# First token tile's logits in two products instead of three, both tiles' meta probabilities in one transpose, and the last square of the feed-forward norm added on POOL

## The chip, the cores and the metric

The kernel runs on one core of a Trainium2 chip. The metric is the device time of one execution in microseconds (us); the median of the runs shown counts.

## What is computed

One decoder block on 256 tokens of width 1024, in float32. 16 learned meta tokens stand ahead, so 272 positions (L) go through the block. What matters here, cut from the reference:

```python
proj = rmsnorm(h, norm_mix_g) @ w_in          # q, k, v, indexer, convolution, gates
# 8 heads of width 128; each query sees the keys that the indexer's top-k selects
logits = einsum('bthd,btkhd->bthk', q_b, k_sel) * HEAD_DIM ** -0.5
p = softmax(where(valid, logits, -inf))
y_attn = einsum('bthk,btkhd->bthd', p, v_sel).reshape(b, l, ATTN_WIDTH) @ w_attn_out
mixed = sigmoid(ga) * y_attn + sigmoid(gb) * y_conv
h = h + mixed @ w_out
f = rmsnorm(h, norm_ffn_g)
h = h + (silu(f @ w_gate) * (f @ w_up)) @ w_down
out = rmsnorm(h, norm_final_g)[:, N_META:]
```

## The kernel before

Weights come in 159 *units*, blocks of 128 rows by 1024 columns, in the order of `UNITS`. For each unit SyncE loads the block (`raw`), ACT copies it to a rounded high part (`whi`, L162), DVE subtracts to get the low part (`wlo`, L170), four units ahead of their use, and TensorE multiplies: high by high, high by low, low by high. All products are of this split kind, which replaces a full float32 product. `narrow` makes three products for each of eight slices of 128 (L248 to L250); `product` makes two, since it multiplies the high weights by high and low of the activations side by side in one product of 512 columns (L281) and adds the two halves later (`total`, L272 and L273).

Nothing schedules: the order of the code is the order on every engine. The attention runs head by head in the units k, q and v of each head. What belongs to an earlier head is hung in behind the unit's products by `behind`: in unit k of head j first `attend(j-2)` (probabilities times values), then `logits(j-1)`; at the start of unit q of head j `normalise` divides the probabilities of head j-1 by their sum; in unit v of head j `values(j-1)` transposes the values and `turned(j-1)` the probabilities. The low parts that `split` makes on DVE wait in a list (`pending`) until the next `ahead` puts them in the queue. So between `turned` of a head and its `attend` TensorE has one unit, the 24 products of the next head's k (for head 6 those of the first gate).

The 256 queries are two tiles of 128: tile 0 sees 144 positions (16 meta and 128), tile 1 all 272. `p` holds both tiles' rows side by side. `side()` hands out the PSUM banks named `misc` in turn, four of them; one bank is 128 partitions by 512 columns. `turned` puts three transposes of 128 by 128 into one bank (`o`, L463) and the two transposes of the 16 meta columns into another (`om`, L466). ACT copies `o` to `pt`, high part; then the meta part twice to `pm` (L471, L472); DVE then subtracts for the low parts of `pt` (L145) and of `pm` (L473). `attend` multiplies values by `pt` (L480, L481), values of the metas by `pm` (L482), then the rest of `pt`.

In the feed-forward part `squares` adds the squares of the eight slices of h on POOL (L652), except that of the last slice; `token_sums` sums it and the last one over partitions on TensorE (L230), behind the first unit of the gate weights.

Of the kernel before, what the change touches and what calls it, by code (L numbers as in the profile page):

```python
# [12 lines left out]
R = mybir.dt.float32r  # L13
# [52 lines left out]
def program(nc, tc, h_in, by_token, params, weights, out):  # L66
# [21 lines left out]
    def side():  # L88
        return misc.tile([P, 512], F32, name="misc")
# [5 lines left out]
    class Pair:  # L95
        def __init__(self, where, shape, name):
            self.hi = where.tile(shape, R, name=name + "_hi")
            self.lo = where.tile(shape, R, name=name + "_lo")

    class Twin:  # L100
        def __init__(self, where, n, name):
            self.both = where.tile([P, KT, 2, n], R, name=name)
# [79 lines left out]
    V.memset(ones, 1.0)  # L182
    act(temp(1), ones, AF.Copy)
    stacks = [(one.tile([64 + META, P], R, name=f"vm{b}"), one.tile([64 + META, S], R, name=f"pm{b}")) for b in range(2)]
    half = one.tile([P, 3], F32, name="half")
    V.memset(half, -0.5)
    h_all = one.tile([P, KT, L], F32, name="h_all")
# [2 lines left out]
    nc.scalar.dma_start(par, params)  # L190
    zeros = temp(S)
    G.memset(zeros, 0.0)
    for pair in stacks:
        for t in pair:
            act(t, zeros[0:64 + META, 0:t.shape[1]], AF.Copy)
# [51 lines left out]
    def three_passes(o, wh, wl, xh, xl, first, last):  # L247
        mm(o, wh, xh, start=first, stop=False)  # L248
        mm(o, wh, xl, start=False, stop=False)  # L249
        mm(o, wl, xh, start=False, stop=last)  # L250
# [158 lines left out]

    def logits():  # L410
        k, q = keep["k"], keep["q"]
        o = side()
        for t in range(2):
            c = slice(t * P, t * P + P)
            three_passes(o[:, OFF[t]:OFF[t] + SEEN[t]], q.hi[:, c], q.lo[:, c], k.hi[:, 0:SEEN[t]], k.lo[:, 0:SEEN[t]],
                         True, True)
        p = three.tile([P, OFF[1] + L], F32, name="p")
        mx = ring.tile([P, 2], F32, name="mx")
        sm = ring.tile([P, 2], F32, name="sm")
        for t in range(2):  # L420
            cols = slice(OFF[t], OFF[t] + SEEN[t])
            V.tensor_tensor_reduce(p[:, cols], o[:, cols], bias[:, cols], 1.0, NEG, OP.add, OP.max, mx[:, t:t + 1])
        V.tensor_tensor(mx, mx, steep[:, 0], OP.mult)
        for t in range(2):
            cols = slice(OFF[t], OFF[t] + SEEN[t])
            act(p[:, cols], p[:, cols], AF.Exp, bias=mx[:, t:t + 1], scale=steep[:, 1, t:t + 1], accum_out=sm[:, t:t + 1])
        keep["p"], keep["sm"] = p, sm

    def normalise():
        p, sm = keep["p"], keep["sm"]  # L430
        V.reciprocal(sm, sm)
        for t in range(2):
            cols = slice(OFF[t], OFF[t] + SEEN[t])
            V.tensor_scalar(p[:, cols], p[:, cols], sm[:, t:t + 1], None, op0=OP.mult)

    def values(h):
        vT = keep.pop("vT")
# [21 lines left out]
    def turned(h):  # L459
        p = keep.pop("p")  # L460
        o = side()
        for i, c in enumerate((META, OFF[1] + META, OFF[1] + META + P)):
            nc.tensor.transpose(o[:, i * P:i * P + P], p[:, c:c + P], ident)  # L463
        om = side()
        for t in range(2):
            nc.tensor.transpose(om[0:META, t * P:t * P + P], p[:, OFF[t]:OFF[t] + META], ident)  # L466
        pt = two.tile([P, 2, 3 * P], R, name="pt")
        pm = stacks[h % 2][1]
        split(pt[:, 0], pt[:, 1], o[:, 0:3 * P])
        om = om[0:META, 0:S]  # L470
        act(pm[0:META], om, AF.Copy)  # L471
        act(pm[64:64 + META], om, AF.Copy)  # L472
        pending.append(lambda: V.tensor_sub(pm[32:32 + META], om, pm[0:META].bitcast(F32)))  # L473
        keep["pt"] = pt

    def attend(h):
# [10 lines left out]
    def step(i):  # L487
        kind, j = UNITS[i]
        final = i == first["wo"] - 1
        if (kind, j) in (("gb", 1), ("ao", 0)):  # L490
            flush()
        if not final:
            ahead(i)
        if kind == "cc":
            o = narrow(i, uT, META - 2)
            some_scores()
            conv_gate(o)
        elif kind == "cu":
            o = narrow(i, uT, META - 2)
            if j == 0:  # L500
                indexer_weights(keep.pop("wi"))
            some_scores()
            if j:
                keep.pop("gated")()
            else:
                indexer_queries(queries[3], 3)
            conv_in(j, o)
        elif kind == "cb":
            o = narrow(i, uT, META)
            some_scores()  # L510
            conv_out(j, o)
        elif kind == "k":
            o = narrow(i, uT)
            behind(j, 0)
            t = temp()
            V.tensor_tensor(t, o, rstd, OP.mult)
            k = Pair(two, [P, L], "k")
            split(k.hi, k.lo, t)
            if j == 0:
                keep.pop("gated")()  # L520
            keep["k"] = k
        elif kind == "q":
            if j:
                normalise()
            o = total(product(i, uT, META)) if j else narrow(i, uT, META)
            q = Pair(two, [P, S], "q")
            split(q.hi, q.lo, o, now=j == 0)
            keep["q"] = q
        elif kind == "v":
            o = narrow(i, uT)  # L530
            behind(j, 2)
            vT = temp(L)
            act(vT, o, AF.Copy)
            keep["vT"] = vT
        elif kind in ("ga", "gb"):
            if (kind, j) == ("gb", 0):
                normalise()
            o = product(i, uT, META) if j > 1 else narrow(i, uT, META)
            if (kind, j) == ("ga", 0):
                behind(H, 0)  # L540
            if (kind, j) == ("ga", 1):
                behind(H, 2)
            t = total(o) if j > 1 else temp(S)
            V.tensor_tensor(t, t if j > 1 else o, rstd[:, META:L], OP.mult)
            act(t, t, AF.Sigmoid)
            keep[kind, j] = t
        elif kind == "co":
            o = product(i, yT(), midway=(lambda: attend(H - 1)) if j == 1 else None)
            t = keep["gb", j]
            V.tensor_tensor(t, t, total(o), OP.mult)  # L550
        elif kind == "ao":
            o = total(product(i, attn())) if j < KT - 1 else narrow(i, attn())
            t = keep.pop(("ga", j))
            V.tensor_tensor(t, t, o, OP.mult)
            V.tensor_tensor(t, t, keep.pop(("gb", j)), OP.add)
            split(mix().hi[:, j], mix().lo[:, j], t, now=final)
        if final:
            ahead(i)
        if steps:
            next(steps.pop(0))  # L560
# [83 lines left out]
    def squares(j, h):  # L644
        if j == 0:
            act(sq_sum, h, AF.Square)
        else:
            sq = temp(S)
            act(sq, h, AF.Square)  # L649
            if j == KT - 1:  # L650
                return sq
            G.tensor_tensor(sq_sum, sq_sum, sq, OP.add)  # L652

    for j in range(KT):
        i = first["wo"] + j
        ahead(i)
        o = product(i, mix()) if j < KT - 1 else narrow(i, mix())
        h = hT[:, j]
        accumulate(h, o)
        act(fT.hi[:, j], by_half(h), AF.Copy, scale=g_ffn[:, j:j + 1])  # L660
        pending.append(lambda j=j, h=h: V.scalar_tensor_tensor(
            fT.lo[:, j], by_half(h), g_ffn[:, j:j + 1], fT.hi[:, j].bitcast(F32), op0=OP.mult, op1=OP.subtract))
        if j == KT - 1:
            flush()
        sq_last = squares(j, h)

    gu = [Apart(one, f"big{b}") for b in range(3)]
    rstd = rstd[:, 0:S]
# [1 line left out]
    for j in range(NF):  # L670
        i = first["gate"] + 2 * j
        ahead(i)
        og = product(i, fT)
        if j == 0:
            o = token_sums([sq_sum, sq_last], B)
            r = ring.tile([P, 2], F32, name="rt")
            for t in range(2):
                V.tensor_scalar(r[:, t:t + 1], o[t][:, 0:1], 1.0 / D, EPS, op0=OP.mult, op1=OP.add)
            G.tensor_tensor(r, r, half[:, 0:2], OP.pow)
            ahead(i + 1)  # L680
            ou = product(i + 1, fT)
            act(rstd, spread(r, B)[:, 0:S], AF.Copy)
        s = total(og)
        V.tensor_tensor(s, s, rstd, OP.mult)
        act(s, s, AF.Silu)  # L685
        G.tensor_tensor(s, s, rstd, OP.mult)  # L686
        if j:
            ahead(i + 1)
            ou = product(i + 1, fT)
        V.tensor_tensor(s, s, total(ou), OP.mult)  # L690
        split(gu[j // KT].hi[:, j % KT], gu[j // KT].lo[:, j % KT], s)
# [113 lines left out]
```

## Time and profile before

| what | value |
|---|---|
| median of 3 runs | 492.08 us (492.07 to 492.34) |
| the profiled execution | 492.07 us |
| its span, first to last instruction | 490.3 us |
| granted TensorE clock, mean | 0.997 |
| busy PE, DVE, ACT, POOL | 483.5, 371.0, 301.0, 74.5 us |

The profiled execution's time is 1.8 us above its span. An engine's busy time is the union of its instructions; matmuls overlap, so what a product costs is read from the distance between the starts of neighbours, not from its duration. L12 is line 12 of the kernel before.

### The profile page before, as it was taken

How to read it: one execution, taken by the hardware profiler on the slowest of the kernel's cores; microseconds unless marked ns; L12 is line 12 of the kernel's file. 1: busy time of each engine (PE TensorE's matmuls, PEld its weight loads, DVE VectorE, ACT ScalarE, POOL GpSimd, SP SyncE). 2: the span in 40 equal slices, each digit the busy share in tenths (PEclk: the TensorE clock that was granted, in tenths of full speed). 3: DMA queues.
4: the chain of work that ended last, by engine and by line, in shares of the span. 5: the costliest groups of instructions: out<-in, count | busy, mean ns of one | idle time of the engine just before them, and what ended most of it. 6: DMA issues, size and time to landing. Idle time of an engine off the chain costs nothing.

```text
span 490.3 us, 8469 instructions
## 1 busy us (share of the span) xinstructions
PE 483.5 (99%) x3215; PEld 444.4 (91%) x3215; DVE 371.0 (76%) x671; ACT 301.0 (61%) x564; POOL 74.5 (15%) x79
## 2 busy tenths in 40 slices
PE   8999999999999999999999999999999999999995
PEld 7999999999999999888888989888888888888895
DVE  4989999968887876887777796887777777664521
ACT  6986475557777777565555565665666666563511
POOL 0034364500000000000000022122111221001110
PEclk9999999999999999999999999999999999999998
DMA  8975476654444444465556554565556655655002
GB/s 303 403 240 184 152 234 195 195 172 139 163 133 151 154 152 140 150 198 177 195 187 185 174 200 172 172 207 193 197 178 190 195 177 200 223 180 167 0 1 86
DMA packets 24696, 87.21 MB, mean 178 GB/s; under 512 B 2880, under 2 KB 3136, under 8 KB 24656
## 3 DMA queue, kind: packets, MB, share of 16 engines
q1 hardware_dynamic: 24368, 86.39, 53.7%
q8 instruction: 25, 0.41, 0.3%
q10 hardware_dynamic: 288, 0.29, 0.2%
q14 instruction: 15, 0.12, 0.1%
HBM read 85.61 MB, written 1.05 MB: 177 GB/s over the span
## 4 chain that ended last, share of the span: by engine, by line
PE 97%; DMA 1%; SPq 0%; DVE 0%; DVEq 0%; ACT 0%; issue 0%
PE acc L281 39%; PE acc L285 20%; PE acc L248 10%; PE acc L250 10%; PE acc L249 10%; DMA raw<-in_weights_dram 1%; PE misc L600 1%; PE misc L604 1%; PE misc L602 1%; PE misc L463 1%; PE misc L249 0%; PE misc L338 0%; PE misc L248 0%; PE misc L339 0%; PE misc L250 0%; PE misc L480 0%
## 5 line engine op out<-in xcount | busy, mean ns | idle before, releaser
L170 DVE TENSOR_TENSOR wlo<-raw,whi 128x1024 fp32r<-128x1024 f32 x155 | 191.6, 1240 | 7.0 <-ACT whi L162 6.5
L281 PE MATMUL acc<-aT,whi 128*128 128x512 f32 x504 | 174.3, 393 | 0.0
L162 ACT ACTIVATE whi<-raw 128x1024 fp32r<-128x1024 f32 x155 | 160.3, 1047 | 0.3 <-PE acc L281 0.3
L285 PE MATMUL acc<-aT,wlo 128*128 128x256 f32 x504 | 131.6, 281 | 0.0
L281 PE MATMUL acc<-big,whi 128*128 128x512 f32 x330 | 115.5, 394 | 0.0
L281 PEld LDWEIGHTS acc<-aT,whi 128*128 128x128 f32 x504 | 91.3, 188 | 16.2
L248 PE MATMUL acc<-aT,whi 128*128 128x272 f32 (+2 forms) x368 | 105.8, 288 | 0.0
L250 PE MATMUL acc<-aT,wlo 128*128 128x272 f32 (+2 forms) x368 | 104.7, 284 | 0.0
L249 PE MATMUL acc<-aT,whi 128*128 128x272 f32 (+2 forms) x368 | 104.4, 284 | 0.0
L285 PEld LDWEIGHTS acc<-aT,wlo 128*128 128x128 f32 x504 | 94.8, 188 | 5.0
L285 PE MATMUL acc<-big,wlo 128*128 128x256 f32 x330 | 88.2, 282 | 0.0
L281 PEld LDWEIGHTS acc<-big,whi 128*128 128x128 f32 x330 | 60.6, 188 | 12.0
L249 PEld LDWEIGHTS acc<-aT,whi 128*128 128x128 f32 x368 | 69.6, 189 | 0.4
L248 PEld LDWEIGHTS acc<-aT,whi 128*128 128x128 f32 x368 | 69.3, 188 | 0.2
L250 PEld LDWEIGHTS acc<-aT,wlo 128*128 128x128 f32 x368 | 69.3, 188 | 0.0
L285 PEld LDWEIGHTS acc<-big,wlo 128*128 128x128 f32 x330 | 62.0, 188 | 2.5
L273 DVE TENSOR_TENSOR temp<-acc,temp 128x256 f32<-128x256 f32 x78 | 33.1, 425 | 39.9 <-ACT temp L272 39.8
L144 ACT ACTIVATE big<-temp 128x256 fp32r<-128x256 f32 x46 | 19.2, 418 | 58.3 <-DVE temp L690 22.5
L652 POOL TENSOR_TENSOR sq_sum<-sq_sum,temp 128x256 f32<-128x256 f32 x12 | 11.0, 918 | 244.5 <-ACT temp L649 244.5
L686 POOL TENSOR_TENSOR temp<-temp,rstd 128x256 f32<-128x256 f32 x22 | 26.0, 1180 | 93.1 <-ACT temp L685 93.1
L272 ACT ACTIVATE temp<-acc 128x256 f32<-128x256 f32 x78 | 29.1, 374 | 10.4 <-PE acc L281 8.3
L145 DVE TENSOR_TENSOR big<-temp,big 128x256 fp32r<-128x256 f32 x46 | 23.1, 503 | 0.5 <-ACT big L144 0.5
(166 smaller groups left out, 483.0 us busy)
## 6 DMA issues: line engine op xcount, KB each, us to landing
raw<-in_weights_dram SPq DMA_DIRECT2D x158, 512.0 KB, 3.5
big<-in_by_token_dram SPq DMA_DIRECT2D x2, 512.0 KB, 9.5
h_all<-in_h_in_dram SPq DMA_DIRECT2D x2, 272.0 KB, 4.2
h_all<-in_h_in_dram SPq DMA_DIRECT2D x1, 544.0 KB, 6.7
raw<-in_weights_dram SPq DMA_DIRECT2D x2, 256.0 KB, 3.7
out_dram<-big SPq DMA_DIRECT2D x2, 256.0 KB, 2.8
out_dram<-big SPq DMA_DIRECT2D x2, 128.0 KB, 1.8
out_dram<-big ACTq DMA_DIRECT2D x1, 256.0 KB, 2.9
```

The source lines that it names most:

```text
L144: act(hi, src, AF.Copy)
L145: low = lambda: V.tensor_sub(lo, src, hi.bitcast(F32))
L162: act(high[i], raw[i], AF.Copy)
L170: V.tensor_sub(lo, raw.pop(i), high[i].bitcast(F32))
L248: mm(o, wh, xh, start=first, stop=False)
L249: mm(o, wh, xl, start=False, stop=False)
L250: mm(o, wl, xh, start=False, stop=last)
L272: act(t, o[:, S:2 * S], AF.Copy)
L273: V.tensor_tensor(t, o[:, 0:S], t, OP.add)
L281: mm(into(o, x), w, x, **kw)
L285: mm(into(o[:, 0:S], x), w, x, **kw)
L686: G.tensor_tensor(s, s, rstd, OP.mult)
```

## The change

The logits of tile 0 are made by one product of 288 columns, the high queries by high and low keys side by side, and one of 144 columns; they have a bank of their own, and the two halves are added outside TensorE: ACT copies the second half to SBUF, POOL adds the bias to it, and the reduction on DVE takes that sum in the place of the bias. Tile 1 is now reduced before tile 0. For that the keys' two parts stand in one tile (`Beside`).

The two tiles' meta probabilities are copied by POOL, after `normalise`, into a tile of 64 columns (`apart`, tile 1 from column 32), which one transpose turns into the fourth quarter of the bank `o`. Two ACT copies and one subtraction of 16 partitions by 256 become four copies and two subtractions of 16 by 128.

In the feed-forward part the last square is added to the sum on POOL too, and `token_sums` gets one term instead of two.

```diff
--- before.py
+++ after.py
@@ -97,6 +97,11 @@
             self.hi = where.tile(shape, R, name=name + "_hi")
             self.lo = where.tile(shape, R, name=name + "_lo")
 
+    class Beside:
+        def __init__(self, where, n, name):
+            self.both = where.tile([P, 2, n], R, name=name)
+            self.hi, self.lo = self.both[:, 0], self.both[:, 1]
+
     class Twin:
         def __init__(self, where, n, name):
             self.both = where.tile([P, KT, 2, n], R, name=name)
@@ -182,6 +187,7 @@
     V.memset(ones, 1.0)
     act(temp(1), ones, AF.Copy)
     stacks = [(one.tile([64 + META, P], R, name=f"vm{b}"), one.tile([64 + META, S], R, name=f"pm{b}")) for b in range(2)]
+    apart = [one.tile([P, 64], F32, name=f"apart{b}") for b in range(2)]
     half = one.tile([P, 3], F32, name="half")
     V.memset(half, -0.5)
     h_all = one.tile([P, KT, L], F32, name="h_all")
@@ -190,6 +196,8 @@
     nc.scalar.dma_start(par, params)
     zeros = temp(S)
     G.memset(zeros, 0.0)
+    for t in apart:
+        G.memset(t, 0.0)
     for pair in stacks:
         for t in pair:
             act(t, zeros[0:64 + META, 0:t.shape[1]], AF.Copy)
@@ -409,17 +417,20 @@
 
     def logits():
         k, q = keep["k"], keep["q"]
-        o = side()
-        for t in range(2):
-            c = slice(t * P, t * P + P)
-            three_passes(o[:, OFF[t]:OFF[t] + SEEN[t]], q.hi[:, c], q.lo[:, c], k.hi[:, 0:SEEN[t]], k.lo[:, 0:SEEN[t]],
-                         True, True)
+        o = [side() for _ in range(2)]
+        n = SEEN[0]
+        mm(halves(o[0][:, 0:2 * n]), q.hi[:, 0:P], k.both[:, :, 0:n], start=True, stop=False)
+        mm(o[0][:, 0:n], q.lo[:, 0:P], k.hi[:, 0:n], start=False, stop=True)
+        three_passes(o[1][:, 0:L], q.hi[:, P:S], q.lo[:, P:S], k.hi, k.lo, True, True)
         p = three.tile([P, OFF[1] + L], F32, name="p")
         mx = ring.tile([P, 2], F32, name="mx")
         sm = ring.tile([P, 2], F32, name="sm")
-        for t in range(2):
+        part = temp(n)
+        act(part, o[0][:, n:2 * n], AF.Copy)
+        G.tensor_tensor(part, part, bias[:, 0:n], OP.add)
+        for t, other in ((1, bias[:, OFF[1]:OFF[1] + L]), (0, part)):
             cols = slice(OFF[t], OFF[t] + SEEN[t])
-            V.tensor_tensor_reduce(p[:, cols], o[:, cols], bias[:, cols], 1.0, NEG, OP.add, OP.max, mx[:, t:t + 1])
+            V.tensor_tensor_reduce(p[:, cols], o[t][:, 0:SEEN[t]], other, 1.0, NEG, OP.add, OP.max, mx[:, t:t + 1])
         V.tensor_tensor(mx, mx, steep[:, 0], OP.mult)
         for t in range(2):
             cols = slice(OFF[t], OFF[t] + SEEN[t])
@@ -432,6 +443,11 @@
         for t in range(2):
             cols = slice(OFF[t], OFF[t] + SEEN[t])
             V.tensor_scalar(p[:, cols], p[:, cols], sm[:, t:t + 1], None, op0=OP.mult)
+
+    two_of = lambda x, n: x.rearrange("p (t c) -> p t c", t=2)[:, :, 0:n]
+
+    def metas_apart(h):
+        G.tensor_copy(two_of(apart[h % 2], META), two_of(keep["p"][:, 0:2 * OFF[1]], META))
 
     def values(h):
         vT = keep.pop("vT")
@@ -461,16 +477,20 @@
         o = side()
         for i, c in enumerate((META, OFF[1] + META, OFF[1] + META + P)):
             nc.tensor.transpose(o[:, i * P:i * P + P], p[:, c:c + P], ident)
-        om = side()
-        for t in range(2):
-            nc.tensor.transpose(om[0:META, t * P:t * P + P], p[:, OFF[t]:OFF[t] + META], ident)
+        om = o[0:64, 3 * P:4 * P]
+        nc.tensor.transpose(om, apart[h % 2], ident)
         pt = two.tile([P, 2, 3 * P], R, name="pt")
         pm = stacks[h % 2][1]
         split(pt[:, 0], pt[:, 1], o[:, 0:3 * P])
-        om = om[0:META, 0:S]
-        act(pm[0:META], om, AF.Copy)
-        act(pm[64:64 + META], om, AF.Copy)
-        pending.append(lambda: V.tensor_sub(pm[32:32 + META], om, pm[0:META].bitcast(F32)))
+        metas = [(slice(t * P, t * P + P), om[32 * t:32 * t + META]) for t in range(2)]
+        for c, of in metas:
+            act(pm[0:META, c], of, AF.Copy)
+            act(pm[64:64 + META, c], of, AF.Copy)
+
+        def low():
+            for c, of in metas:
+                V.tensor_sub(pm[32:32 + META, c], of, pm[0:META, c].bitcast(F32))
+        pending.append(low)
         keep["pt"] = pt
 
     def attend(h):
@@ -514,7 +534,7 @@
             behind(j, 0)
             t = temp()
             V.tensor_tensor(t, o, rstd, OP.mult)
-            k = Pair(two, [P, L], "k")
+            k = Beside(two, L, "k")
             split(k.hi, k.lo, t)
             if j == 0:
                 keep.pop("gated")()
@@ -522,6 +542,7 @@
         elif kind == "q":
             if j:
                 normalise()
+                metas_apart(j - 1)
             o = total(product(i, uT, META)) if j else narrow(i, uT, META)
             q = Pair(two, [P, S], "q")
             split(q.hi, q.lo, o, now=j == 0)
@@ -535,6 +556,7 @@
         elif kind in ("ga", "gb"):
             if (kind, j) == ("gb", 0):
                 normalise()
+                metas_apart(H - 1)
             o = product(i, uT, META) if j > 1 else narrow(i, uT, META)
             if (kind, j) == ("ga", 0):
                 behind(H, 0)
@@ -647,8 +669,6 @@
         else:
             sq = temp(S)
             act(sq, h, AF.Square)
-            if j == KT - 1:
-                return sq
             G.tensor_tensor(sq_sum, sq_sum, sq, OP.add)
 
     for j in range(KT):
@@ -662,7 +682,7 @@
             fT.lo[:, j], by_half(h), g_ffn[:, j:j + 1], fT.hi[:, j].bitcast(F32), op0=OP.mult, op1=OP.subtract))
         if j == KT - 1:
             flush()
-        sq_last = squares(j, h)
+        squares(j, h)
 
     gu = [Apart(one, f"big{b}") for b in range(3)]
     rstd = rstd[:, 0:S]
@@ -672,7 +692,7 @@
         ahead(i)
         og = product(i, fT)
         if j == 0:
-            o = token_sums([sq_sum, sq_last], B)
+            o = token_sums([sq_sum], B)
             r = ring.tile([P, 2], F32, name="rt")
             for t in range(2):
                 V.tensor_scalar(r[:, t:t + 1], o[t][:, 0:1], 1.0 / D, EPS, op0=OP.mult, op1=OP.add)
```

The order shows the two places at which engines wait. First DVE, from the low parts of the values and probabilities of one head to the reduction of the next head's logits, with the semaphores that a row waits for in brackets (Activation is ACT, Pool is POOL). Before:

```order
L455 SCALAR_TENSOR_TENSOR v_lo<-misc,mean,v_hi 128x128 [waits Activation_49]
L455 SCALAR_TENSOR_TENSOR v_lo<-misc,mean,v_hi 128x128
L455 SCALAR_TENSOR_TENSOR vm_90<-misc,mean,vm_90 16x128
L145 TENSOR_TENSOR pt<-misc,pt 128x384 [waits Activation_49]
L473 TENSOR_TENSOR pm_91<-misc,pm_91 16x256 [waits PE_49,Activation_49]
L273 TENSOR_TENSOR temp<-misc,temp 128x256 [waits Activation_49]
L422 ISA p,mx<-misc,bias 128x144 [waits PE_49]
L422 ISA mx 128x1
L422 ISA p,mx<-misc,bias 128x272
```

and with the change:

```order
L471 SCALAR_TENSOR_TENSOR v_lo<-misc,mean,v_hi 128x128 [waits Activation_49]
L471 SCALAR_TENSOR_TENSOR v_lo<-misc,mean,v_hi 128x128
L471 SCALAR_TENSOR_TENSOR vm_90<-misc,mean,vm_90 16x128
L150 TENSOR_TENSOR pt<-misc,pt 128x384 [waits PE_49,Activation_49]
L492 TENSOR_TENSOR pm_91<-misc,pm_91 16x128 x2
L281 TENSOR_TENSOR temp<-misc,temp 128x256 [waits Activation_49]
L433 ISA p,mx<-misc,bias 128x272 [waits PE_49]
L433 ISA mx 128x1
L433 ISA p,mx<-misc,temp 128x144 [waits Pool_49]
```

The subtraction for `pm` had a wait of its own; now both subtractions for `pm` have none, and what they need is waited for one row earlier, at that for `pt`: in the built program the number of ACT instructions that this row waits for is reached by the fourth copy to `pm` (L488, tile 1); before, it was reached by the copy to `pt` itself. Tile 0's reduction now waits for POOL.

Second ACT, from the transposed probabilities of one head to the exponentials of the next. Before:

```order
L144 ACTIVATE pt<-misc 128x384 [waits PE_49]
L471 ACTIVATE pm_91<-misc 16x256 [waits PE_49]
L472 ACTIVATE pm_91<-misc 16x256
L533 ACTIVATE temp<-acc 128x272
L162 ACTIVATE whi<-raw 128x1024 [waits DMAHW3_49,Activation_49]
L272 ACTIVATE temp<-misc 128x256 [waits PE_49,Pool_49]
L144 ACTIVATE big_1723<-temp 128x256 [waits DVE_49]
L426 ACTIVATE p,sm<-p,mx,steep 128x144 [waits DVE_49]
```

and with the change:

```order
L149 ACTIVATE pt<-misc 128x384 [waits PE_49]
L487 ACTIVATE pm_89<-misc 16x128
L488 ACTIVATE pm_89<-misc 16x128
L487 ACTIVATE pm_89<-misc 16x128
L488 ACTIVATE pm_89<-misc 16x128
L554 ACTIVATE temp<-acc 128x272
L167 ACTIVATE whi<-raw 128x1024 [waits DMAHW0_49,Activation_49]
L280 ACTIVATE temp<-misc 128x256 [waits PE_49,Pool_49]
L149 ACTIVATE big_1730<-temp 128x256 [waits DVE_49]
L429 ACTIVATE temp<-misc 128x144 [waits PE_49,Pool_49]
L437 ACTIVATE p,sm<-p,mx,steep 128x144 [waits DVE_49]
```

Two copies became four, and the copy of tile 0's second half (L429) stands behind the high part of the previous head's output (L149), which waits for DVE.

## Rows read from the trace of the kernel before

**Rows 1.** The page, chain of work that ended last: share of the span by engine.

```profile
PE 97%; DMA 1%; SPq 0%; DVE 0%; DVEq 0%; ACT 0%; issue 0%
```

**Rows 2.** Busy times in one head's stretch, start and end in us, then engine by engine.

```profile
139.80:150.90 11.10, 11.10 (x84) 10.64 (x84) 8.96 (x22) 8.59 (x20) 0.00 (x0) 1.00 0.47 146
```

**Rows 3.** Timeline of PE, one head's logits: start us, us, engine, line, operation.

```profile
139.76 0.23 PE L248 MATMUL misc<-k_hi,q_hi 128*128 128x144 f32 x1
...
140.05 0.33 PE L248 MATMUL misc<-k_hi,q_hi 128*128 128x272 f32 x1
...
140.47 0.40 PE L281 MATMUL acc<-aT,whi 128*128 128x512 f32 x1
```

**Rows 4.** Timeline of PE, the same head's meta transposes and the next products.

```profile
146.95 0.38 PE L466 MATMUL misc<-ident,p 128*16 128x128 f32 x2
...
147.30 0.29 PE L249 MATMUL acc<-aT,whi 128*128 128x272 f32 x1
```

**Rows 5.** Timeline of ACT behind these transposes; in brackets idle before it and releaser.

```profile
146.88 0.62 ACT L450 ACTIVATE v_hi<-misc,mean 128x128 fp32r<-128x128 f32 x2 [0.67 <-PE misc L441]
147.40 0.34 ACT L450 ACTIVATE vm<-misc,mean 16x128 fp32r<-16x128 f32 x1
...
148.15 0.49 ACT L144 ACTIVATE pt<-misc 128x384 fp32r<-128x384 f32 x1
148.53 0.36 ACT L471 ACTIVATE pm<-misc 16x256 fp32r<-16x256 f32 x1
```

**Rows 6.** Timeline of DVE there, the low parts.

```profile
148.16 0.61 DVE L455 SCALAR_TENSOR_TENSOR v_lo<-misc,mean,v_hi 128x128 fp32r<-128x128 f32 x2 [0.68 <-ACT vm L451]
...
149.15 0.56 DVE L145 TENSOR_TENSOR pt<-misc,pt 128x384 fp32r<-128x384 f32 x1
149.74 0.41 DVE L473 TENSOR_TENSOR pm<-misc,pm 16x256 fp32r<-16x256 f32 x1
```

**Rows 7.** Timeline of PE, `attend` with the metas and the next logits.

```profile
150.20 0.39 PE L480 MATMUL misc<-pt,v_hi 128*128 128x512 f32 x1
...
150.55 0.28 PE L482 MATMUL misc<-pm,vm 80*128 80x256 f32 x1
...
150.91 0.23 PE L248 MATMUL misc<-k_hi,q_hi 128*128 128x144 f32 x1
```

**Rows 8.** Timelines of ACT and DVE behind the logits of rows 3.

```profile
140.83 0.42 ACT L144 ACTIVATE big<-temp 128x256 fp32r<-128x256 f32 x1 [0.49 <-DVE temp L273]
141.61 0.51 ACT L426 ACTIVATE p<-p,mx,steep 128x144 f32<-128x144 f32 x1 [0.36 <-DVE mx L423]
...
140.71 0.30 DVE L422 CUSTOM_DVE_ANT_0 p<-misc,bias 128x144 f32<-128x144 f32 x1
...
141.42 0.16 DVE L423 TENSOR_TENSOR mx<-mx,steep 128x2 f32<-128x2 f32 x1
...
143.86 0.56 DVE L434 TENSOR_SCALAR p<-p,sm 128x144 f32<-128x144 f32 x2
```

**Rows 9.** Groups by line with shapes kept apart: busy us, mean ns, idle before.

```profile
L652 POOL TENSOR_TENSOR sq_sum<-sq_sum,temp 128x256 f32<-128x256 f32 x12 | 11.0, 918 | 244.5 <-ACT temp L649 244.5
L397 POOL TENSOR_TENSOR temp<-temp 128x256 f32<-128x256 f32 x8 | 10.5, 1312 | 29.6 <-ACT temp L395 29.6
...
L341 ACT ACTIVATE temp<-misc 128x144 f32<-128x144 f32 x8 | 2.0, 291 | 0.1
```

**Rows 10.** Timelines of ACT, POOL and PE at the feed-forward norm.

```profile
295.19 0.40 ACT L649 ACTIVATE temp<-h_all 128x256 f32<-128x256 f32 x1
...
297.54 0.40 ACT L649 ACTIVATE temp<-h_all 128x256 f32<-128x256 f32 x1
...
295.73 0.74 POOL L652 TENSOR_TENSOR sq_sum<-sq_sum,temp 128x256 f32<-128x256 f32 x1 [2.06 <-ACT temp L649]
...
298.59 0.28 PE L230 MATMUL acc<-ones,sq_sum 128*128 128x1 f32 x2
...
299.40 0.48 PE L281 MATMUL acc<-aT,whi 128*128 128x512 f32 x1
```

## The prediction

> **What bounds the kernel.** I read the chain of waits first: TensorE (PE) holds 97% of it [rows 1], so a product saved anywhere is time saved, and whatever stops PE is time lost. Then the stretch of one head: PE is busy for all 11.10 us, DVE for 8.96, ACT for 8.59, POOL not at all [rows 2]. So there is room for more work on the other engines; what has to be asked is whether it lies on a path that ends at a PE instruction with little to spare. For that I read the timelines of one head, engine by engine: its logits at 139.76, its transposes from 146.3 to 147.1, its `attend` from 150.20. All times below are of that head; its neighbours repeat it. A time with the mark "then" is one with the change.
>
> **What PE gains.** Six logits products take 140.47 - 139.76 = 0.71 us [rows 3]. A product of 272 columns costs 0.126: there are 23 from 147.30 to `attend` at 150.20 [rows 4, 7]. That leaves (0.71 - 0.378) / 3 = 0.111 for one of 144. With the change 288 columns cost 0.126 x 288 / 272 = 0.133, then 0.111, then 0.378: 0.62 in all, 0.09 saved. The two meta transposes with one product of 272 behind them take 0.35 [rows 4], so a transpose costs 0.11, and one goes. Per head 0.20, for eight heads 1.6 us. Bounds: nothing (the wider moving side costs what the third product did) and 0.22 (two full steps of 0.11).
>
> In the feed-forward part eight small matmuls (a float32 product shows as two) take 299.40 - 298.59 = 0.81 us [rows 10]; half go, 0.40. But PE now waits for POOL's add of the last square. The square ends at 297.54 + 0.40 = 297.94; POOL follows ACT after 0.14 (295.59 to 295.73) and takes 0.74, so the sum is there at 298.82 [rows 10]. With another 0.15 to start PE again (I take that handover, for PE never waits on DVE or POOL in these rows) the first matmul moves from 298.59 to 298.97: 0.38 lost. I put this part at 0, from -0.4 (hidden) to +0.6 (an add of 1.31, the dearest POOL row [rows 9]).
>
> **What the other engines get: the bank.** The meta transpose now lies in the bank of the other three. In the order, DVE's subtraction for `pt` waits until ACT has made all four copies to `pm`, because both engines read that bank; the two subtractions for `pm` stand behind it. The trace shows that such a wait is real: the low parts of the values, which need only `v_hi`, start at 148.16 after 0.68 idle, released by the last copy that ACT makes out of the values' bank (`vm` L451) [rows 6]. The Trainium skill states the rule (PSUM — Partial Sum Buffer, section "PSUM bank collisions raise a hardware error"): two engines may not touch one bank in the same 32 partitions at once, reads against reads included, so software has to put one behind the other. By that rule, and by the row, sharing the bank costs an ordering that two banks did not.
>
> Its price: copies of 16 partitions by 128 columns follow each other every 0.375 us (147.40 to 148.15 for two); the first to `pm` starts at 148.53 [rows 5]. Four of them end 3 x 0.375 + 0.36 = 1.49 later, at 150.02. DVE takes `pt` at 150.05 instead of 149.15, starts on `pm` 0.59 later as now (149.15 to 149.74 [rows 6]), at 150.64, and needs 0.37 + 0.34 for the two halves (I take ACT's spacing and length for that size, since DVE's are not among the rows): 151.35. PE's `L482` reads `pm`; it runs at 150.55 now [rows 7], where `pm` is ready at 150.15. Then 151.35 + 0.15 = 151.50. ACT's chain would start 0.09 earlier, with the transposes: 151.41, so 0.86 late. PE cannot go past this: the rest of `attend`, the next logits and the next unit stand behind it on its queue. 0.86 is net of what that head saves on PE.
>
> **What the other engines get: tile 0's sum.** ACT's copy of the second half stands behind the high part of the previous output, 140.83 to 141.25 [rows 8]; with 0.05 overlap it runs from 141.20 for 0.29 (the 128x144 copy out of PSUM [rows 9]) to 141.49. POOL starts at 141.63. Its add of 144 columns is in no row; 256 cost 0.74 at best [rows 10], 0.92 and 1.31 on average at two lines [rows 9]. Bounds 0.41 (0.74 by columns alone) and 1.31; I take 0.48, near the quickest row, since DVE has nothing to do meanwhile. So 142.11 then. DVE reduces tile 0 from 142.15 (0.30 and its read-out), multiplies at 142.50, and the exponentials start 0.19 later as now (141.42 to 141.61): 142.69 against 141.61 [rows 8], 1.08 late. DVE idles for nearly 1 us in front of tile 0's reduction; behind it are the scaling of k, three weight splits, `normalise`, q's parts. Weight splits are four units ahead, more than a head's 11.10 us, so PE does not feel those. But ACT, in the same order, reaches the copy of the values later: it now waits 0.67 for the transposes [rows 5], which covers only that much of 1.08. With transposes 0.09 earlier it starts at 146.88 - 0.67 + 1.08 = 147.29, 0.50 behind them, and everything of the part above moves by 0.50: `L482` at 151.91 then, 1.36 late.
>
> The new POOL copy of the metas is hidden: `normalise` ends at 143.86 + 0.56 + 1.08 = 145.50 then [rows 8]; with 0.14 and at most 0.74 POOL is done at 146.38, PE wants it at about 146.86 (146.95 less 0.09). An add of 1.31 would use that up. The zeroing of two small tiles at the start stands ahead of the identity, in a stretch where POOL only prepares; I take nothing, and at most two adds of 144 columns, 0.96, once.
>
> **Sum.** `attend` of heads 0 to 6 comes one unit after its transposes; head 7 has more units between and only gains. Head 0 has no earlier output ahead of its logits, so ACT is free: 0.86. Heads 1 to 6: 6 x 1.36 = 8.16. Head 7: -0.20. Feed-forward: 0. Together +8.8 on the profiled 492.07 (span 490.3 and 1.8 around it; the median is 492.08): 500.9 us. The stall comes back in each head, since PE's own pace from logits to transposes is unchanged.
>
> **Rivals.** *The bank alone*: POOL and ACT are quick enough for ACT to be back in time. For it: 0.41 for the add and slack of 0.67. Then 7 x 0.86 - 0.20 = 5.8, 497.9; if the small copies also follow each other every 0.26, as the 128-partition ones do (146.88 to 147.40 for two [rows 5]), 0.35 less per head: 495.4. *The late sum alone*: DVE's `pt` isn't held up by the meta copies. Against it: the wait in the order and the row of 0.68. DVE would take `pt` at 149.56, end `pm` at 150.86, `L482` at 151.01, 0.46 late: 6 x 0.46 - 0.20 = 2.6, 494.6. *It does what it says*: neither path reaches PE, 1.6 saved and up to 0.4 more, 490.5. It decides at `L482`: `pm` must be ready by 150.20. Against it: `pt` alone, held by four copies, is done at 150.5, and PE wants it at 150.00 already. *A dear POOL*: 1.31 for the add, 0.83 more in six heads, 505.9; a fall of the granted clock in PE's new gaps would look alike in time.
>
> **Chances.** The forecast 0.58, the bank alone 0.20, the late sum alone 0.07, it does what it says 0.06, dearer 0.09. A measurement here tells 0.2% (1 us) from no change. Faster 0.06; between, 0.02, out of the two cheap cases; slower 0.92. The range leaves out the faster case, the late sum and the dearest: 495.5 to 503.
>
> **What would show it.** In the new trace: PE idle before L500 (on DVE's `pt`, L150) and before L502 (on `pm`, L492), together over 1 us in each of seven heads; `pt`'s subtraction on DVE released by ACT L488; DVE idle by about 1 us before tile 0's reduction, released by POOL L430; the values' copy on ACT with no idle before it. No idle on PE at the transposes. If PE stays busy through `attend`, the forecast is wrong at the bank; if ACT still idles before L466, at the late sum.

## The result, and the profile after

| what | before | changed |
|---|---|---|
| median of four runs each, same chip | 492.21 us (492.07 to 492.58) | 499.16 us (498.93 to 499.36) |
| ratio, 95% interval | 1 | 1.0142 (1.0129 to 1.0154) |
| span of the profiled execution | 490.3 us | 497.2 us |
| granted TensorE clock, mean | 0.997 | 0.996 |

Slower by 6.95 us; the forecast was 8.8 slower (500.9, range 495.5 to 503.0). The page of the changed kernel, its first part and the shares of the chain of work that ended last, against [rows 1]:

```profile
PE 485.4 (98%) x3195; PEld 443.0 (89%) x3195; DVE 372.3 (75%) x679; ACT 304.4 (61%) x588; POOL 82.5 (17%) x98
...
PE 77%; DVE 11%; ACT 6%; issue 3%; DMA 1%; POOL 1%; SPq 0%; DVEq 0%; ACTq 0%; POOLq 0%
```

PE held 97% of the chain and now holds 77%: DVE and ACT have come into it with 17%. That share tells who stands on the path, not what was lost: 17% of the span would be 85 us. What waits is in the view of the waits (engine, tile and line, what it waits for: us in all, times, longest us):

```profile
DVE p L433 <- POOL temp L430: 6.2, 7, 0.9
DVE pt L150 <- ACT pm L488: 4.6, 8, 0.6
...
PE misc L500 <- DVE pt L150: 2.6, 6, 0.6
...
PE acc L238 <- POOL sq_sum L672: 1.2, 1, 1.2
...
PE acc L289 <- DVE big L150: 0.8, 1, 0.8
```

The first two are off PE's queue but lead to the third. The timelines of one head, engine by engine, of the changed kernel (start us, us, engine, line, operation, idle before it and its releaser), against [rows 5 to 8]:

```profile
143.41 0.49 POOL L430 TENSOR_TENSOR temp<-temp,bias 128x144 f32<-128x144 f32 x1 [7.63 <-ACT temp L429]
...
143.94 0.31 DVE L433 CUSTOM_DVE_ANT_0 p<-misc,temp 128x144 f32<-128x144 f32 x1 [0.88 <-POOL temp L430]
...
148.99 0.61 ACT L466 ACTIVATE v_hi<-misc,mean 128x128 fp32r<-128x128 f32 x2
...
150.63 0.25 ACT L487 ACTIVATE pm<-misc 16x128 fp32r<-16x128 f32 x1
150.90 0.27 ACT L488 ACTIVATE pm<-misc 16x128 fp32r<-16x128 f32 x1
151.19 0.27 ACT L487 ACTIVATE pm<-misc 16x128 fp32r<-16x128 f32 x1
151.48 0.27 ACT L488 ACTIVATE pm<-misc 16x128 fp32r<-16x128 f32 x1
...
151.78 0.56 DVE L150 TENSOR_TENSOR pt<-misc,pt 128x384 fp32r<-128x384 f32 x1 [0.57 <-ACT pm L488]
152.37 0.58 DVE L492 TENSOR_TENSOR pm<-misc,pm 16x128 fp32r<-16x128 f32 x2
...
152.40 0.50 PE L500 MATMUL misc<-pt,v_hi 128*128 128x512 f32 x1 [0.38 <-DVE pt L150]
...
153.10 0.36 PE L502 MATMUL misc<-pm,vm 80*128 80x256 f32 x1
...
153.52 0.30 PE L422 MATMUL misc<-k,q_hi 128*128 128x288 f32 x1
```

DVE stands idle for 0.57 us ahead of `pt`, until the last of ACT's four copies has ended (151.75), and everything on PE stands behind `pm`: the product with the metas starts 0.15 after the second subtraction ends (152.95). Listed from head to head, that product's start says how the lag grows:

| head | 0 | 1 | 2 | 3 | 4 | 5 | 6 | 7 |
|---|---|---|---|---|---|---|---|---|
| before, `L482` | 117.25 | 128.34 | 139.41 | 150.55 | 161.63 | 172.72 | 183.65 | 198.68 |
| changed, `L502` | 117.43 | 129.36 | 141.23 | 153.10 | 164.97 | 176.82 | 188.69 | 203.59 |
| later by | 0.18 | 1.02 | 1.82 | 2.55 | 3.34 | 4.10 | 5.04 | 4.91 |

A head takes 11.88 instead of 11.07 us. At the first product behind the sums of the feed-forward part the lag is 6.94 (306.34 against 299.40 [rows 10]). The 2.03 that come behind head 7 are in two places. These are the rows of PE there, and of the engines that lead to them:

```profile
201.63 0.56 DVE L150 TENSOR_TENSOR pt<-misc,pt 128x384 fp32r<-128x384 f32 x1 [0.57 <-ACT pm L488]
...
204.60 0.42 ACT L567 ACTIVATE temp<-temp 128x256 f32<-128x256 f32 x1 [1.61 <-DVE temp L566]
...
205.99 0.39 ACT L280 ACTIVATE temp<-misc 128x256 f32<-128x256 f32 x1
...
208.87 0.51 PE L289 MATMUL acc<-big,whi 128*128 128x512 f32 x1 [0.78 <-DVE big L150]
...
304.01 1.22 DVE L175 TENSOR_TENSOR wlo<-raw,whi 128x1024 fp32r<-128x1024 f32 x1
...
304.03 1.79 POOL L672 TENSOR_TENSOR sq_sum<-sq_sum,temp 128x256 f32<-128x256 f32 x1 [1.61 <-ACT temp L671]
...
305.87 0.61 PE L238 MATMUL acc<-ones,sq_sum 128*128 128x1 f32 x4 [1.17 <-POOL sq_sum L672]
```

In head 7 the held `pt` puts DVE's whole queue back, the gate's product with `rstd` (L566) among it; ACT waits 1.61 for that, and takes head 7's output out of PSUM (L280) 2.75 after `attend` began (203.24), where before it took 1.65:

```profile
198.33 0.40 PE L480 MATMUL misc<-pt,v_hi 128*128 128x512 f32 x1
...
199.98 0.36 ACT L272 ACTIVATE temp<-misc 128x256 f32<-128x256 f32 x1
```

The first unit of the attention's output waits for it: its products lag by 4.91 ahead of that wait and by 5.96 behind it. In the feed-forward part POOL's add took 1.79, not 0.74.

### The profile page after: what moved, and what is told of

Same layout as the page of the kernel before. It is cut to its first block, busy times and chain, and to the rows that moved or that the text cites. A ratio compares the mean times of both kernels' runs of the same rounds, so it can differ in the third digit from the quotient of the medians.

```text
span 497.2 us, 8498 instructions
## 1 busy us (share of the span) xinstructions
PE 485.4 (98%) x3195; PEld 443.0 (89%) x3195; DVE 372.3 (75%) x679; ACT 304.4 (61%) x588; POOL 82.5 (17%) x98
## 3 DMA queue, kind: packets, MB, share of 16 engines
HBM read 85.61 MB, written 1.05 MB: 174 GB/s over the span
## 4 chain that ended last, share of the span: by engine, by line
PE 77%; DVE 11%; ACT 6%; issue 3%; DMA 1%; POOL 1%; SPq 0%; DVEq 0%; ACTq 0%; POOLq 0%
PE acc L289 33%; PE acc L293 17%; PE acc L256 7%; PE acc L258 7%; PE acc L257 7%; DVE wlo L175 4%; DVE temp L281 1%; DMA raw<-in_weights_dram 1%; DVE aT L681 1%; ACT whi L167 1%; DVE pt L150 1%; ACT pm L488 1%; PE misc L500 1%; DVE p L445 1%; ACT pm L487 1%
## 5 line engine op out<-in xcount | busy, mean ns | idle before, releaser
L149 ACT ACTIVATE big<-temp 128x256 fp32r<-128x256 f32 x46 | 19.2, 418 | 58.9 <-DVE temp L710 22.5
L672 POOL TENSOR_TENSOR sq_sum<-sq_sum,temp 128x256 f32<-128x256 f32 x13 | 12.8, 985 | 154.3 <-ACT temp L671 154.3
L280 ACT ACTIVATE temp<-acc 128x256 f32<-128x256 f32 x78 | 29.2, 374 | 10.2 <-PE acc L289 8.2
```

The lines of the kernel that those rows point to most:

```text
L149: act(hi, src, AF.Copy)
L280: act(t, o[:, S:2 * S], AF.Copy)
```

## The experiments

Differences are to the kernel before in the same runs (492.06, 492.13 or 492.21), with the 95% interval of the ratio. The first four undo parts of the change.

**The metas in a bank of their own.**

```diff
-        om = o[0:64, 3 * P:4 * P]
+        om = side()[0:64, 0:P]
```

> The change with one thing undone: the meta transpose gets a bank of its own again (one transpose, four copies, two subtractions stay). If it is the shared bank that holds DVE's subtraction for the probabilities, this comes 0.57 us earlier in each head, PE's idle time ahead of L500 goes, about 0.2 us stays ahead of L502 in heads 1 to 6, and the 1 us wait behind head 7 goes: some 4.6 us less than the change, 494.6. Rival, volume: if the time is lost to the larger number of instructions on ACT and DVE, whatever bank they read, nothing moves: 499.2.

495.07 us, +3.01 (1.0047 to 1.0077), 0.5 more than expected. The bank costs 3.94 of the 6.95. Its timelines of DVE and PE, same head:

```profile
150.05 0.56 DVE L150 TENSOR_TENSOR pt<-misc,pt 128x384 fp32r<-128x384 f32 x1
150.64 0.58 DVE L492 TENSOR_TENSOR pm<-misc,pm 16x128 fp32r<-16x128 f32 x2
...
150.67 0.50 PE L500 MATMUL misc<-pt,v_hi 128*128 128x512 f32 x1
...
151.37 0.36 PE L502 MATMUL misc<-pm,vm 80*128 80x256 f32 x1
```

`pt` has no idle before it any more, though ACT still makes four copies. What is left is a late chain: `pm` still ends only 0.15 ahead of its product, and a head takes 11.33 us. PE's wait behind head 7 falls from 0.78 to 0.23.

**The logits of before**: six products, one bank, the reduction with the bias.

```diff
-        mm(halves(o[0][:, 0:2 * n]), q.hi[:, 0:P], k.both[:, :, 0:n], start=True, stop=False)
...
-        act(part, o[0][:, n:2 * n], AF.Copy)
-        G.tensor_tensor(part, part, bias[:, 0:n], OP.add)
```

> The change with its logits undone (three products for each tile in one bank, no copy on ACT and no add on POOL). If the late sum delays ACT's copy of the values by the 0.40 us that the trace of the change shows between the transposes and it, heads 1 to 6 get that back and lose 0.09 each on PE: some 2 us less than the change, 497.0. Rival, the sum is innocent because the shared bank alone sets the end: 0.7 us more than the change, from eight products: 499.9.

497.90 us, +5.84 (1.0102 to 1.0132). ACT's timeline shows that it is back in time for the values:

```profile
148.36 0.62 ACT L463 ACTIVATE v_hi<-misc,mean 128x128 fp32r<-128x128 f32 x2 [0.50 <-PE misc L454]
```

So the late sum costs 1.11 net of what PE saves, about half of the 2 us that I expected, and the bank is enough for most of the loss: with it PE's wait behind head 7 stays at 0.73.

**The feed-forward part of before.**

```diff
+            if j == KT - 1:
+                return sq
-            o = token_sums([sq_sum], B)
+            o = token_sums([sq_sum, sq_last], B)
```

> The change with its feed-forward part undone (the last square is summed on TensorE again). The trace of the change shows PE idle for 1.17 us ahead of the sums, on a POOL add that took 1.79 us instead of 0.74. If that idle time is on the path, 1.0 us less than the change: 498.2. Rival, another wait takes its place at once (the weights of the next unit): no difference, 499.2.

498.11 us, +6.05 (1.0105 to 1.0139). POOL's last add costs 0.90; the trace of the changed kernel had 0.98 there.

**Own bank and the logits of before** (the first two edits together; what stays is the one transpose and POOL's last add).

> The change with the bank and the logits both undone; the one transpose for the metas and the feed-forward part stay. If the two waits together are the whole loss in the attention, PE has no idle time there, the transpose saves 0.11 us per head, 0.9 us, and the feed-forward part costs 1.0: 492.2 to 492.6, no change against the kernel before. Rival, volume on ACT and DVE: above 494.

493.69 us, +1.63 (1.002 to 1.0046): over 1 us more than expected, and just short of the rival's 494. A head takes 11.10 us, against 11.07 before. The transpose that is saved gives nothing, since `pm`, with two more copies and one more subtraction ahead, is now only just ready: its product starts 0.14 after it. Of the 1.63, 0.90 is the add of the square, and 0.43 is the wait before the attention's output: the products lag by 0.42 ahead of it and by 0.85 behind it (0.20 of idle). The 0.42 are not the heads': 0.40 of it is there at head 0's first logits (106.90, against 106.50 before), with nothing changed on PE ahead of them. The profiled executions scatter by as much there: 106.61 and 106.92 in the two runs below with the new logits alone, whose programs are the same up to that point. Against this kernel the late sum costs 1.38, and against the logits of before the bank costs 4.21: the two hardly help or hinder each other.

Then each saving by itself, with its cost hidden.

**The new logits alone, the halves added on DVE** (an edit of the kernel before; metas and feed-forward part as before).

```diff
+        V.tensor_tensor(p[:, 0:n], o[0][:, n:2 * n], bias[:, 0:n], OP.add)
+        for t, other in ((0, p[:, 0:n]), (1, bias[:, OFF[1]:OFF[1] + L])):
```

> The kernel before with the new logits alone (288 columns and 144), but tile 0's second half added by DVE itself, ahead of the reduction, instead of by ACT and POOL. DVE works about 0.3 us more per head and the exponentials come 0.3 us later, within the 0.67 us that ACT idles ahead of the values. If PE's saving of 0.09 us per head was sized right and only the hand-overs ate it, 0.7 us less than the kernel before: 491.4. Rival, the wide product saves PE nothing: 492.1, or later if 0.3 us on DVE already reaches PE.

491.39 us, -0.82 (0.9974 to 0.9992). The saving of 0.09 a head, 0.7 in all, is real. DVE's timeline: the added row costs one instruction of 0.30 and no handover.

```profile
140.50 0.30 DVE L426 TENSOR_TENSOR p<-misc,bias 128x144 f32<-128x144 f32 x1
140.83 0.31 DVE L429 CUSTOM_DVE_ANT_0 p<-misc,p 128x144 f32<-128x144 f32 x1
```

**The same logits, the halves added by ACT and POOL as in the change.**

```diff
+        act(part, o[0][:, n:2 * n], AF.Copy)
+        G.tensor_tensor(part, part, bias[:, 0:n], OP.add)
```

> The kernel before with the new logits alone, as the change has them: ACT copies, POOL adds. By the prediction's rival, the late sum alone, 0.46 us per head are lost: 494.6. By the trace of the change, where DVE reaches the probabilities 3.17 us behind the first transpose of the values, the low part of the metas would be ready 0.06 us late at most, and PE saves 0.09: 491.9, no change.

492.29 us, +0.08 (0.9993 to 1.0011). The way over ACT and POOL, with tile 1 reduced first, costs 0.90 against DVE's, all of the saving and no more. With the transposes of before the late chain only just reaches PE (DVE ends `pt` at 150.28, 0.16 ahead of its product), by 0.13 a head: 11.09 against 10.96 with the sum on DVE.

**Both savings in the attention, hidden**: own bank, sum on DVE, the product with the metas last in its group; feed-forward part as before.

```diff
-        mm(o[:, 0:S], vm, pm, start=False, stop=False)
-        mm(halves(o)[:, :, P:S], v.hi[:, P:S], pt[:, :, S:S + P], start=False, stop=True)
+        mm(halves(o)[:, :, P:S], v.hi[:, P:S], pt[:, :, S:S + P], start=False, stop=False)
+        mm(o[:, 0:S], vm, pm, start=False, stop=True)
```

> All of the attention's part of the change with its waits taken away: tile 0's second half added by DVE, the one meta transpose in a bank of its own, the product with the metas moved to the end of its group (0.24 us more for the low part of the metas); the feed-forward part undone. If the two waits were all that stood against the saving, PE has no idle time in the attention and 0.20 us per head are gained: 490.5. Rival, the two extra copies on ACT and the extra subtraction on DVE still come too late: no idle time removed beyond that of the run with its own bank and old logits, 491.5 to 492.5.

491.11 us, -1.10 (0.9969 to 0.9987): faster than both kernels, and between what I expected and the rival. A head takes 10.87 us, 0.20 less than before, which is the sum worked out for PE. That would be 1.6 for eight heads; a wait of the kind seen behind head 7 takes some of it back. PE's products are 1.52 earlier than before ahead of it, and 1.07 behind it:

```profile
201.84 0.72 PE L289 MATMUL acc<-big,whi 128*128 128x512 f32 x2 [0.19 <-DVE big L150]
```

**The same with the last square added on DVE.**

```diff
+            (V if j == KT - 1 else G).tensor_tensor(sq_sum, sq_sum, sq, OP.add)
```

> The run with the attention's waits taken away, with the feed-forward part of the change put back but its last add given to DVE instead of POOL. The add takes 0.42 us behind the low part of the last slice; PE waits 0.1 us for it and saves 0.40: 0.3 us less than that run, 490.8. Rival, the sums are late on DVE too, and PE waits as long as it saves: 491.1.

491.03 us, -1.10 (0.9967 to 0.9986), no different from the one before. Timelines of DVE and PE:

```profile
296.72 0.42 DVE L670 TENSOR_TENSOR sq_sum<-sq_sum,temp 128x256 f32<-128x256 f32 x1
...
297.28 0.58 PE L238 MATMUL acc<-ones,sq_sum 128*128 128x1 f32 x4
```

From the last product ahead of the sums to the first behind them PE takes 0.72 (297.00 to 297.72), against 1.04 in the run without this edit (297.26 to 298.30): the 0.3 that was expected. The spans are shorter (median 488.9 against 489.3), but the time around the span is longer by nearly as much (2.1 against 1.8). Why, stays open; as a gain of the whole time this one is inconclusive. The profiled executions differ by more (488.6 against 489.2), since this one is 0.29 earlier already at head 0's first logits (106.27 against 106.56), which the edit doesn't touch.

The last two ask what made POOL's add 1.79 long.

**A small memset on DVE ahead of its weight split**, so that POOL's add starts first.

```diff
+    V.memset(scratch[:, 0, 0:S], 0.0)
```

> The change with one instruction more: DVE clears 256 columns of a tile that is no longer used, right behind the low part of the last slice, so that the next weight split on DVE starts some 0.2 us later, behind the start of POOL's add. If the add took 1.79 us because DVE's split, which began 0.02 us earlier, kept POOL from reading, the add takes about 0.74 again, the split takes longer instead, and PE's wait falls from 1.17 to about 0.3 us: 0.9 us less than the change, 498.3. Rival, the add is slow for another reason (ACT's copies, its place): no change, 499.2.

501.11 us, +8.90 (1.0159 to 1.0188). Not the quick add that I had expected. POOL, DVE and PE, then the windows (start and end, us, busy us of PE, PEld, DVE, ACT and POOL, granted clock, DMA share, GB/s):

```profile
304.46 2.00 POOL L672 TENSOR_TENSOR sq_sum<-sq_sum,temp 128x256 f32<-128x256 f32 x1 [1.61 <-ACT temp L671]
...
304.53 0.27 DVE L686 MEMSET scratch<- 128x256 f32 x1
304.72 1.16 DVE L175 TENSOR_TENSOR wlo<-raw,whi 128x1024 fp32r<-128x1024 f32 x1
...
306.51 0.60 PE L238 MATMUL acc<-ones,sq_sum 128*128 128x1 f32 x4 [1.42 <-POOL sq_sum L672]
```

```profile
307.40:310.60 3.20, 3.20 (x13) 2.72 (x12) 1.06 (x1) 0.00 (x0) 1.63 (x1) 0.51 0.72 225
```

The add started 0.26 ahead of the split and still ended 0.58 behind it, as in the changed kernel (0.59: 305.82 against 305.23). What this can't tell is whether the split alone held it, for the memset began only 0.07 behind the add and lay between the two. The longer gap alone is some 0.3 us. The rest is the clock: 0.9 us after a gap of 1.42 us on PE the granted clock fell, and stood at 0.51, the 1.2 GHz level, for over 3 us. Three of the four runs lie at 501.06 to 501.22 with a mean clock of 0.992 or 0.993, the fourth at 499.54 with 0.999.

**The weight split behind the add**: a copy of one column on DVE that waits for the sum.

```diff
+    V.tensor_copy(scratch[:, 0, 0:1], sq_sum[:, 0:1])
```

> The change with one instruction more: DVE copies one column of POOL's sum, right behind the low part of the last slice, so that its next weight split cannot begin before POOL's last add has ended. If it is DVE's split that holds the add (in the two runs looked at, the add ended 0.59 and 0.58 us behind the split's end), the add takes 0.6 to 0.75 us, PE's wait falls from 1.17 to about 0.2, and the split's 0.8 us of delay is hidden by the four units ahead: 498.2. Rival, something else holds POOL (ACT's copies of that moment): the add stays near 1.8 us and the time at 499.2.

498.22 us, +6.09 (1.011 to 1.0137), 0.86 less than the change:

```profile
304.44 0.75 POOL L672 TENSOR_TENSOR sq_sum<-sq_sum,temp 128x256 f32<-128x256 f32 x1 [1.61 <-ACT temp L671]
...
305.24 0.61 PE L238 MATMUL acc<-ones,sq_sum 128*128 128x1 f32 x4 [0.16 <-POOL sq_sum L672]
...
305.29 1.22 DVE L175 TENSOR_TENSOR wlo<-raw,whi 128x1024 fp32r<-128x1024 f32 x1
```

With the split moved behind it, and ACT's copies where they were, the same add takes 0.75. So DVE's split holds POOL's add.

## Why the prediction was right, and where its sizes were off

**The mechanism held.** `pt` on DVE is released by ACT's fourth copy (0.57 idle, all eight heads), tile 0's reduction by POOL (0.88 idle, "nearly 1 us"), the values' copy on ACT has no idle before it, PE has none at the transposes, and the stall comes back in each of heads 1 to 6. One sign was missed: PE was to idle ahead of L500 and L502 for over 1 us in each of seven heads, but the rows show 0.38 and 0.10 in the head looked at, and in head 0 PE didn't wait ahead of L500. The own bank alone gives 3.94 back, the old logits alone 1.11: both paths that were added are there, the bank the dearer. The rule on one bank and two engines (the Trainium skill, PSUM — Partial Sum Buffer, section "PSUM bank collisions raise a hardware error") agrees with the rows as far as they go: the wait for ACT's copies is there with the shared bank and gone with the own one. What happens without that wait no run here shows.

**What PE gains** was right: 0.09 a head for the logits gives 0.7, and 0.82 was measured; both savings 0.20, and a head is 0.20 shorter once all is hidden.

**The stall of 1.36 a head was 0.81.** The mis-sized term is the price of the copies to `pm`. Step by step in the head of rows 2 to 8, PE's logits to the next logits:

| stretch | before | forecast | measured |
|---|---|---|---|
| logits to the start of the values' transposes | 6.53 | 6.44 | 6.41 |
| from there to ACT's copy of the values | 0.59 | 1.09 | 0.92 |
| from there to the product with `pm` | 3.67 | 4.62 | 4.11 |
| from there to the next logits | 0.36 | 0.36 | 0.42 |
| sum | 11.15 | 12.51 | 11.86 |

The third row is 0.51 less than forecast. I had taken 0.375 from one copy to the next and 0.36 for the last, from copies of the same size that scale by `mean`, a value per partition read from memory (`vm` in [rows 5]); these plain ones start every 0.28 and the last takes 0.27, so the fourth ends at 151.75, 1.12 after the first began, instead of 1.49. The two subtractions take 0.58 instead of 0.71. The spacing of 0.26 that stood in the rival of the bank alone was the nearer price. The second row is 0.17 less: ACT was late by 0.33, not 0.50. POOL's add itself was right, 0.49 for 0.48, as was the copy of the metas, hidden with 0.21. This head takes 0.71 more than before; the six together lost 4.86 (0.81 each, since before the others take a little less than this one, 11.07 on average), not 8.16. Head 0 lost 0.18 instead of 0.86; 0.51 of that is the same chain, and 0.13 is no saving: the profiled execution stood that much earlier at head 0's first logits already (106.37, against 106.50 before).

**Head 7 was taken too lightly.** "Only gains" held for `attend`, -0.13 for -0.20, but I stopped there: the held `pt` delays what stands behind it on DVE, and the first unit of the attention's output waits. 1.05 lost between head 7's product with `pm` and the first unit of the feed-forward gates (301.77 against 295.81), all of it at the one wait shown. The idle time in that row is only 0.78, because products overlap: their starts are put off by more than the time in which PE stands still. What is queued behind the held instruction was asked for heads 0 to 6 and not for the one whose `attend` had time.

**The feed-forward part was put at 0 and costs 0.98** (0.90 by its own experiment), outside the range of -0.4 to +0.6 given for it. PE's first sum came 1.32 late instead of 0.38, and the four small products left save 0.34 instead of 0.40. The add's 0.74 came from the one row in [rows 10], and 1.31 was the dearest mean; the add that PE waits for took 1.79, since DVE was splitting weights meanwhile. The trace of before had the other side of it, in DVE's timeline: the row L661 took 0.96 beside POOL's add of 0.74, and 0.48 where POOL was still. The weight split ahead of it overlapped that add only in its last 0.14 us.

```profile
294.65 1.22 DVE L170 TENSOR_TENSOR wlo<-raw,whi 128x1024 fp32r<-128x1024 f32 x1
295.79 0.96 DVE L661 SCALAR_TENSOR_TENSOR aT<-h_all,par,aT 128x256 fp32r<-128x256 f32 x1
...
297.67 0.48 DVE L661 SCALAR_TENSOR_TENSOR aT<-h_all,par,aT 128x256 fp32r<-128x256 f32 x1 [0.58 <-ACT aT L660]
```

The Trainium skill (SBUF — State Buffer, section "Who interferes with whom") says that a DVE instruction with two inputs in SBUF contends with a GpSimd (POOL) instruction that reads SBUF. The two trials above agree. By the same section the order of issue decides which of the two blocks; that fits the row of before, but not plainly the trial in which POOL's row began 0.26 ahead of the split's and was held all the same. Whether the memset between them held it first, or POOL reads later than its row begins, no run here separates.

Together: heads 0.18 + 4.86 - 0.13, behind them 1.05, the sums 0.98: 6.94 of the 6.95. So 8.8 came as near as it did because a stall sized 4.0 us too high in heads 0 to 6 was partly made up by two losses, 2.0 together, that the sum lacked: that the total came near is luck, beyond the mechanism.

**The rivals.** The bank alone is nearest to the run with the old logits: without the 0.90 of the square it stands at about 497.0, between its two prices of 497.9 and 495.4. The late sum alone is nearest to the run with its own bank: about 494.2 without the square, for 494.6; but there a head lost 0.26 and not 0.46, and 0.49 was lost behind head 7. With the transposes of before, the late sum cost no more than the logits saved (492.29). The fall of the clock, named with the dear POOL, did not come in the changed kernel (0.996) but came, in three of four executions, when its gap was lengthened from 1.17 to 1.42 us.

## What to carry to other kernels

A PSUM bank that two engines read put one of them behind the other here: to save a transpose of 0.11 us by packing it into a bank that ACT reads in four steps cost 0.5 us a head, while the same transpose into a bank of its own, with the product that needs it put last and the sum left to DVE, let the saving through. Ask where a partial sum is finished: the engine that reads the result anyway took 0.30 us for it, two other engines used up the whole gain. For an add on POOL read the duration off a row that has the same DVE work beside it, and follow a held instruction's queue to its end in every stage, also where the first consumer has time.

## What the runs showed of the hardware

- POOL's add of 128x256 took 0.74 and 0.75 us with no weight split of DVE beside it but the last 0.14 us of one, and 1.79 and 2.00 with one of 1.22 and 1.16, ending 0.58 to 0.59 after that ended, though it began first in one of them (with a memset of DVE between).
- Plain ACT copies of 16x128 out of PSUM took 0.25 to 0.27 us and started every 0.28; those that scale by a value from memory took 0.34 to 0.36 and started every 0.375.
- After 1.42 us without products the granted clock was at the 1.2 GHz level for 3 us in the profiled run, which took 1.7 us longer than the one run of that kernel whose mean clock showed no fall (0.999). After 1.17 us it stayed at full speed.
- The stretch ahead of the first head, with the same program on PE, ended up to 0.3 us earlier or later from one profiled execution to another (head 0's first logits at 106.27 and 106.56, at 106.61 and 106.92).
